# A hybrid decoder block on one core: the attention's value products in two halves of their PSUM bank, and a reordered head

## The chip, the core and the metric

The kernel runs on one core of a Trainium2 chip. A core has five engines that this text names: PE (TensorE, the matrix products; its weight loads, PEld, overlap them), DVE (VectorE), ACT (ScalarE), POOL (GpSimd) and SP, whose queue issues the transfers (DMAs). Matrix products are written to PSUM, a memory that this kernel uses in banks of 128 partitions x 512 fp32 values, and DVE and ACT read them there; the other tiles lie in SBUF. The metric is the device time in microseconds (us) of one execution, less is better.

## The reference

One layer on x of 1024 tokens x 1024 channels, in fp32. h = RMSNorm(x) is projected with one matrix `w_in` to some 13,900 columns, which feed three branches; each branch is projected back to 1024 channels, the three are weighted by sigmoid gates and summed, projected once more, added to x and normalised.

- Mamba-2 branch: a causal convolution over tokens of width 4 with SiLU gives x, B and C; step sizes dt = softplus(...); a scan in chunks of 128 tokens; a SiLU gate and an RMSNorm.
- Pooling branch: trailing means over 2, 4, 8, 16 tokens, a small linear map, a SiLU gate.
- Attention branch, 16 heads of 64, stick-breaking instead of a softmax:

```python
z = jnp.einsum('bhtd,bhsd->bhts', qb, kb) * scale
log_beta = log_sigmoid(z)
log_one_minus = where(causal, log_sigmoid(-z), 0.0)
later = lax.cumsum(log_one_minus, axis=3, reverse=True) - log_one_minus
att = where(causal, exp(log_beta + later), 0.0)
o = einsum('bhts,bhsd->bhtd', att, vb)      # then o * silu(gate)
```

## The kernel before, in words

Every fp32 product is made of parts: an operand is split into a high part (a rounding cast, ACT) and a low part (operand minus high, DVE), and the products high x high, high x low and low x high are summed in PSUM. The stages run one after the other: the head (convolution part, `conv_part`), attention (`attention_part`), the chunked scan, pooling, merge and output.

**The head.** `norm_in` normalises and transposes x to `hT` (eight tiles). `conv_gen(b)` projects one block of 256 columns to four PSUM tiles (two column tiles `ct` x two token halves), convolves each over tokens (ACT L684, three DVE instructions L689), and after the second half takes the SiLU: ACT sigmoid L692, then the product L693 on POOL, then a DMA. `zd_open` (L597, L598, DVE) splits the weights of the 32 step sizes; `dt_part` multiplies them with h and works out dt and its sums: in `conv_gen(1)` it is advanced twice (L621 to L638, then L642 to L651), and the rest, two transposes L656, a copy L658 and two DMAs, is run by `self.drain(dt)` right after. Afterwards `g_gen(1)` projects a gate block (ACT sigmoid L774, DVE product L775). From then on blocks are multiplied with seven products instead of eight (`seven_block`, L291), which needs sums of token halves: `seven_operands` (L230 to L249, DVE) makes them, and `t_split` splits each one (ACT copy L256, DVE subtraction L257). In the whole head the order on PE, DVE, POOL and ACT is that in which the program writes the instructions. The PSUM tiles of the projections rotate over two banks (`mm`) and three more (`mmx`); the first seven-product block begins in a bank that the third gate product L775 reads.

**Attention.** A unit is (pair of heads p, head hd, pair of query tiles ip), ip = 0 to 3, 64 units. For the two query tiles of a unit `stage_qk` makes the scores (L879 to L882), two sigmoids of them (ACT L883, L886), the running product over the keys from the end (DVE scan L888) and the weights (DVE L889); rows get longer with ip, up to 1024 keys. `stage_tr(u, jc)` transposes a 256 x 256 block of weights (L906) and splits it into the tile `attT` (ACT L908, DVE L909). `stage_av(u, jc)` multiplies it with v (L929), four products into 256 columns of the bank `av`: columns 0 to 255 for even ip, 256 to 511 for odd ip. After the last one of an odd ip the bank is emptied: ACT copies 64 of its partitions to `o` (L934), DVE adds the other 64 (L935), POOL multiplies with the gate `gt` (L936), a DMA stores it. The bank is then given to the next group (ip = 2 after 1, the next head's ip = 0 after 3).

The program writes PE's order out by hand: in unit m it places the scores of unit m + 1 at the first two steps, and after each step a share of projection work for later heads (`fill`), so that PE has work while ACT, DVE and POOL do theirs. A value step comes four transposes after its own (`late`). Per head there are ten of each; unit ip = 0 has two steps, then four, six and eight. The other engines' order in the attention is set by the scheduler of the framework, which also sets every wait between engines, from the tiles and the PSUM banks that instructions touch.

## Time and profile before

| what | value |
|---|---|
| median of 3 runs | 2102.17 us (2101.26 to 2102.92) |
| the profiled execution: time, span | 2102.4 us, 2100.6 us |
[...]
| PE busy | 2037.3 us, 97% |
| DVE, ACT, POOL busy | 1325.7, 947.4, 311.2 us |

The span is the time from the first to the last instruction. [...] Where a line of a profile names a releaser (`<-`), that instruction ended the wait. A merged line (`x3`) gives the start of the first and the time to the end of the last of so many instructions.

### The profile page before, as it was taken

The numbers are of one execution on the slowest core, as the hardware profiler recorded it, in microseconds if no ns is written. First come the engines' busy times: TensorE is split into PE (matmuls) and PEld (weight loads), VectorE is DVE, ScalarE is ACT, GpSimd is POOL, SyncE is SP. The second block draws the span as 40 slices with busy tenths as digits, with TensorE's granted clock in tenths as the row PEclk, the third lists the DMA queues.
The fourth block names the chain that finished last, engine by engine and source line by source line (L and its number), as shares of the span: only waits on it lengthen the run. The fifth ranks groups of instructions, "written<-read, shape, count | busy, mean of one in ns | idle before, by whom it ended". The sixth has DMA issues, their size and how long they took to land.

```text
span 2100.6 us, 29502 instructions
## 1 busy us (share of the span) xinstructions
PE 2037.3 (97%) x11312; PEld 1735.0 (83%) x11312; DVE 1325.7 (63%) x1821; ACT 947.4 (45%) x1921; POOL 311.2 (15%) x416
## 2 busy tenths in 40 slices
PE   8999999999999999999999899999999999999998
PEld 6878878788888788988887787777888888888898
DVE  6786888748667757665667736777747724425333
ACT  5343344335545545454545546666543413313131
POOL 3000000001111201010101124444200002221000
PEclk9999999999999899999999999999999999999999
DMA  5322233331121121211111165666563635433232
GB/s 197 103 86 100 91 110 113 134 114 49 46 66 39 48 66 56 60 57 58 53 59 53 61 185 190 208 198 195 164 211 128 215 99 171 143 128 110 81 131 81
DMA packets 116155, 233.99 MB, mean 111 GB/s; under 512 B 9776, under 2 KB 59696, under 8 KB 116016
## 3 DMA queue, kind: packets, MB, share of 16 engines
q1 hardware_dynamic: 116016, 232.12, 34.1%
q8 instruction: 89, 1.46, 0.3%
q14 instruction: 50, 0.41, 0.1%
HBM read 168.38 MB, written 63.70 MB: 110 GB/s over the span
## 4 chain that ended last, share of the span: by engine, by line
PE 78%; DVE 15%; ACT 3%; issue 3%; DMA 1%; DVEq 0%; POOL 0%; ACTq 0%; SPq 0%; POOLq 0%
PE mm L388 26%; PE mmx L388 14%; PE mm L397 12%; PE mmx L291 4%; DVE om L888 4%; PE mmx L397 4%; PE av L929 3%; DVE acc L350 3%; PE yd L1157 3%; PE tr L906 2%; PE mm L291 1%; DVE be L889 1%; PE yo L1160 1%; PE st L1163 1%; PE z L879 1%
## 5 line engine op out<-in xcount | busy, mean ns | idle before, releaser
L388 PE MATMUL mm<-hT,w 128*128 128x512 f32 x2232 | 590.2, 408 | 2.9 <-DVE hT L584 2.8
L388 PEld LDWEIGHTS mm<-hT,w 128*128 128x128 f32 x2232 | 409.7, 191 | 94.4 <-issue 15.1
L397 PE MATMUL mm<-w,hT 128*128 128x256 f32 x2112 | 291.2, 288 | 1.1 <-issue 1.1
L397 PEld LDWEIGHTS mm<-w,hT 128*128 128x128 f32 x2112 | 268.7, 193 | 1.8 <-issue 1.3
L388 PE MATMUL mmx<-x,w 128*128 128x512 f32 x1008 | 230.3, 389 | 0.0
L129 DVE TENSOR_TENSOR w<-raw,w 128x1024 fp32r<-128x1024 f32 x116 | 152.1, 1313 | 119.4 <-ACT w L128 119.1
L388 PEld LDWEIGHTS mmx<-x,w 128*128 128x128 f32 x1008 | 189.2, 188 | 39.3
L888 DVE TENSOR_TENSOR_SCAN om<-om,zero 128x128 f32<-128x128 f32 (+7 forms) x128 | 174.0, 1360 | 68.1 <-ACT om L883 67.2
L908 ACT CAST attT<-tr 128x512 fp32r<-128x512 f32 (+2 forms) x224 | 98.2, 438 | 159.9 <-PE tr L906 106.3
L909 DVE TENSOR_TENSOR attT<-tr,attT 128x512 fp32r<-128x512 f32 (+2 forms) x224 | 111.2, 497 | 91.2 <-ACT attT L908 90.0
L128 ACT CAST w<-raw 128x1024 fp32r<-128x1024 f32 x116 | 121.5, 1050 | 66.1 <-PE mmx L388 27.4
L883 ACT ACTIVATE om<-z 128x128 f32<-128x128 f32 (+2 forms) x192 | 92.5, 495 | 76.7 <-PE z L882 75.5
L388 PE MATMUL mm<-x,w 128*128 128x512 f32 x528 | 122.7, 389 | 0.0
L1286 ACT ACTIVATE gt<-gt 128x1024 f32<-128x1024 f32 x32 | 34.0, 1062 | 185.7 <-DMA gt<-d_gate 185.0
L388 PEld LDWEIGHTS mm<-x,w 128*128 128x128 f32 x528 | 99.1, 188 | 20.7
L388 PE MATMUL mmx<-hT,w 128*128 128x512 f32 x456 | 104.9, 390 | 0.0
L889 DVE TENSOR_TENSOR be<-be,om 128x128 f32<-128x128 f32 (+7 forms) x128 | 97.3, 760 | 11.9
L1134 POOL TENSOR_TENSOR E<-E,cbm 128x1024 f32<-128x1024 f32 x32 | 76.6, 2393 | 160.0 <-issue 104.8
L388 PEld LDWEIGHTS mmx<-hT,w 128*128 128x128 f32 x456 | 85.4, 188 | 17.6
L906 PE MATMUL tr<-cm,be 128*128 128x128 f32 x576 | 93.0, 280 | 0.5 <-DVE be L889 0.5
L886 ACT ACTIVATE be<-z 128x128 f32<-128x128 f32 (+2 forms) x192 | 92.5, 500 | 0.1
L870 POOL MEMSET om<- 128x1 f32 x128 | 12.6, 98 | 503.9 <-DVE be L889 405.1
(250 smaller groups left out, 3296.0 us busy)
## 6 DMA issues: line engine op xcount, KB each, us to landing
raw<-in_wblk SPq DMA_DIRECT2D x148, 512.0 KB, 4.1
E<-d_act SPq DMA_DIRECT2D x32, 512.0 KB, 4.8
gt<-d_gate SPq DMA_DIRECT2D x32, 512.0 KB, 3.9
d_gate<-mg SPq DMA_DIRECT2D x16, 512.0 KB, 4.0
xi<-d_x SPq DMA_DIRECT2D x32, 256.0 KB, 3.2
zs<-d_z SPq DMA_DIRECT2D x32, 256.0 KB, 2.7
d_ssm<-yt SPq DMA_DIRECT2D x32, 256.0 KB, 3.1
xraw<-d_ssm SPq DMA_DIRECT2D x16, 512.0 KB, 5.9
```

Of the source, the lines that this page charges most:

```text
L128: nc.scalar.copy(hi, raw)
L129: nc.vector.tensor_tensor(out=lo, in0=raw, in1=hi.bitcast(F32), op=ALU.subtract)
L291: T.matmul(ps, w[a](i, k), mov[b](j, k), start=first and n == 0, stop=n == 11, skip_group_check=not first)
L388: T.matmul(ps, w(a, k, ct * P, ct * P + P), mov(b, k, half * 512, half * 512 + 512), start=n == 0, stop=n == 23)
L397: T.matmul(ps, sta(a, k, tok * P, tok * P + P), w(b, k, 0, ncol), start=n == 0, stop=n == 23)
L883: A.activation(om[:, c0 : c0 + n], z[:, 0:n], AF.Sigmoid, scale=-0.125)
L886: A.activation(be[:, c0 : c0 + n], z[:, 0:n], AF.Sigmoid, scale=0.125)
L888: V.tensor_tensor_scan(out=rev, data0=rev, data1=self.zero.broadcast_to((P, L)), initial=1.0, op0=ALU.mult, op1=ALU.add)
L889: V.tensor_tensor(out=be[:, 0:L], in0=be[:, 0:L], in1=om[:, 1 : L + 1], op=ALU.mult)
L906: T.transpose(tr[:, c : c + P], b[:, (2 * jc + j) * P : (2 * jc + j + 1) * P], self.ident)
L908: A.copy(at[:, 0, sl], tr[:, sl])
L909: V.tensor_tensor(out=at[:, 1, sl], in0=tr[:, sl], in1=at[:, 0, sl].bitcast(F32), op=ALU.subtract)
```

## The change

- `t_split` only puts the low part's subtraction on a list; `t_flush` issues it, one or two instructions into the next token sum, at the first step of `conv_gen(1)`, or at step 50 of `g_gen(1)`.
- The SiLU product of `conv_gen` runs on DVE instead of POOL (four instructions).
- The last part of `dt_part` is run 15 products into `g_gen(1)` instead of ahead of it; the memory of `ws` is opened there.
- The bank `av` is one tile for the whole attention. Even ip write its first half and odd ip the second, and each half is emptied as soon as its own ip is complete (ACT copy and DVE addition of 256 columns, 64 times, instead of 512 columns, 32 times). `o` has two buffers and is taken at the first step of a group.
- A value step comes three transposes after its own instead of four, and `attT` has four buffers instead of five.

```diff
@@ -215,6 +215,7 @@
         self.tt = {i: pool.tile([P, 2, 4, 512], F32R, name=f"tt{i}") for i in (2, 3)}
         self.park = self.dram.tile([P, 4, 2, 512], F32, name="d_b12")
         self.t1, keep = {}, {}
+        self.t_late = []
         lo, hi = slice(0, 512), slice(512, 1024)
         f = lambda t, part, sl: t[:, part, sl].bitcast(F32)
 
@@ -229,6 +230,7 @@
             e = keep[k] = epool.tile([P, 512], F32, tag="te", name="te", bufs=2) if k < 2 else tmp("te")
             V.tensor_tensor(out=d, in0=f(a, 0, hi), in1=f(a, 0, lo), op=ALU.subtract)
             V.tensor_tensor(out=t1, in0=f(a, 1, hi), in1=f(a, 1, lo), op=ALU.subtract)
+            self.t_flush()
             V.tensor_tensor(out=t1, in0=t1, in1=d, op=ALU.add)
             V.tensor_tensor(out=e, in0=f(c, 0, hi), in1=t1, op=ALU.subtract)
             V.tensor_tensor(out=e, in0=e, in1=f(c, 1, hi), op=ALU.add)
@@ -238,6 +240,7 @@
             a, c = self.hT[k], self.hT[4 + k]
             d, e = tmp("td"), tmp("te")
             V.tensor_tensor(out=d, in0=f(c, 0, hi), in1=f(a, 0, hi), op=ALU.subtract)
+            self.t_flush()
             V.tensor_tensor(out=e, in0=f(c, 1, hi), in1=f(a, 1, hi), op=ALU.subtract)
             V.tensor_tensor(out=d, in0=d, in1=e, op=ALU.add)
             self.t_split(3, k, d)
@@ -246,6 +249,7 @@
             c = self.hT[4 + k]
             d, e = tmp("td"), keep.pop(k)
             V.tensor_tensor(out=d, in0=f(c, 0, lo), in1=e, op=ALU.subtract)
+            self.t_flush()
             V.tensor_tensor(out=d, in0=d, in1=f(c, 1, lo), op=ALU.add)
             self.t_split(4, k, d)
 
@@ -254,7 +258,11 @@
     def t_split(self, i, k, src):
         hi, lo = self.tt[i][:, 0, k], self.tt[i][:, 1, k]
         self.nc.scalar.copy(hi, src)
-        self.nc.vector.tensor_tensor(out=lo, in0=src, in1=hi.bitcast(F32), op=ALU.subtract)
+        self.t_late.append(lambda: self.nc.vector.tensor_tensor(out=lo, in0=src, in1=hi.bitcast(F32), op=ALU.subtract))
+
+    def t_flush(self):
+        while self.t_late:
+            self.t_late.pop(0)()
 
     def seven_first(self):
 
@@ -690,7 +698,7 @@
             if half == 1:
                 sg = pool.tile([P, S], F32, tag="csg", name="csg", bufs=2)
                 nc.scalar.activation(sg, acc[:, 0:S], AF.Sigmoid)
-                nc.gpsimd.tensor_tensor(out=sg, in0=sg, in1=acc[:, 0:S], op=ALU.mult)
+                nc.vector.tensor_tensor(out=sg, in0=sg, in1=acc[:, 0:S], op=ALU.mult)
                 dst = self.d_x[col // 4][:, col % 4] if col < 16 else self.d_bc[:, col - 16]
                 nc.sync.dma_start(out=dst, in_=sg)
             yield
@@ -730,18 +738,22 @@
                 if i in steps:
                     steps[i][0](steps[i][1])
             for i, _ in enumerate(self.conv_gen(1, pool)):
+                if i == 0:
+                    self.t_flush()
                 if i in (0, 2):
                     next(dt, None)
-            self.drain(dt)
-            dctx.close()
-            self.wspool = self.sb(ctx, "ws_sb", 2)
             self.wseven = {}
             steps = {4: (two, 2), 16: (one, 3), 32: (three, 3), 44: (two, 3)}
             prep = {}
             for i, _ in enumerate(self.g_gen(1)):
                 if i in steps:
                     steps[i][0](steps[i][1])
+                if i == 14:
+                    self.drain(dt)
+                    dctx.close()
+                    self.wspool = self.sb(ctx, "ws_sb", 2)
                 if i == 50:
+                    self.t_flush()
                     prep = self.seven_prep(BLK[SEVEN[0]])
                 if i > 50 and i % 8 == 0 and prep:
                     prep.pop(min(prep))()
@@ -850,7 +862,7 @@
             self.mmx = 0
             pz = self.ps(ctx, "a_z", 3)
             ptr = self.ps(ctx, "a_tr", 2)
-            pav = self.ps(ctx, "a_av", 1)
+            avs = self.ps(ctx, "a_av", 1).tile([P, 512], F32, name="av")
             qk, vv = {}, {}
             make = {"vz": lambda p: self.vz_gen(p, pool, vv), "qk": lambda p: self.qk_gen(p, pool, qk), "z": self.z_gen, "g": self.g_gen, "m": self.merge_gen}
             self.start_fill([(key, make[key[0]](key[1])) for key in [("vz", 0), ("qk", 0)] + sum(ATT_FILL, [])])
@@ -896,7 +908,7 @@
                 ip = u[2]
                 b0, b1 = state[u, 0], state[u, 1]
                 tr = ptr.tile([P, 512], F32, tag="tr", name="tr")
-                at = pool.tile([P, 2, 512], F32R, tag="attT", name="attT", bufs=5)
+                at = pool.tile([P, 2, 512], F32R, tag="attT", name="attT", bufs=4)
                 blocks = [(0, 0, b0), (0, 1, b1), (1, 0, b0), (1, 1, b1)]
                 if jc == ip:
                     blocks.pop(2)
@@ -917,24 +929,26 @@
                 rows = slice(64 * hd, 64 * hd + 64)
                 half = ip // 2
                 hs = slice(half * 512, half * 512 + 512)
-                if jc == 0 and ip % 2 == 0:
-                    gt = pool.tile([P, 512], F32, tag="gt", name="gt", bufs=1)
-                    nc.sync.dma_start(out=gt[rows], in_=self.d_g[rows, p, hs])
-                    av[0] = (pav.tile([P, 512], F32, tag="av", name="av"), gt)
-                ps, gt = av[0]
-                c = 256 * (ip % 2)
+                if jc == 0:
+                    if ip % 2 == 0:
+                        gt = pool.tile([P, 512], F32, tag="gt", name="gt", bufs=1)
+                        nc.sync.dma_start(out=gt[rows], in_=self.d_g[rows, p, hs])
+                        av[1] = (pool.tile([P, 512], F32, tag="o", name="o", bufs=2), gt)
+                ps = avs[:, 256 * (ip % 2) : 256 * (ip % 2) + 256]
+                o, gt = av[1]
                 n = 0
                 for j in range(2):
                     for part in range(2):
-                        T.matmul(ps[:, c : c + 256], v[:, 2 * jc + j], at[:, part, 256 * j : 256 * j + 256], start=jc == 0 and n == 0, stop=jc == ip and n == 3)
+                        T.matmul(ps, v[:, 2 * jc + j], at[:, part, 256 * j : 256 * j + 256], start=jc == 0 and n == 0, stop=jc == ip and n == 3)
                         n += 1
-                if jc == ip and ip % 2 == 1:
+                if jc == ip:
                     other = slice(64 - 64 * hd, 128 - 64 * hd)
-                    o = pool.tile([P, 512], F32, tag="o", name="o", bufs=1)
-                    A.copy(o[rows], ps[other])
-                    V.tensor_tensor(out=o[rows], in0=o[rows], in1=ps[rows], op=ALU.add)
-                    G.tensor_tensor(out=o[rows], in0=o[rows], in1=gt[rows], op=ALU.mult)
-                    nc.sync.dma_start(out=self.d_y["sb"][p // 4][rows, p % 4, hs], in_=o[rows])
+                    cs = slice(256 * (ip % 2), 256 * (ip % 2) + 256)
+                    A.copy(o[rows, cs], ps[other])
+                    V.tensor_tensor(out=o[rows, cs], in0=o[rows, cs], in1=ps[rows], op=ALU.add)
+                    if ip % 2 == 1:
+                        G.tensor_tensor(out=o[rows], in0=o[rows], in1=gt[rows], op=ALU.mult)
+                        nc.sync.dma_start(out=self.d_y["sb"][p // 4][rows, p % 4, hs], in_=o[rows])
 
             n = len(units)
             weight = [0.4 + 0.6 * (u[2] + 1) / 2.5 for u in units]
@@ -950,7 +964,7 @@
                 for jc in range(ip + 1):
                     subs.append((stage_tr, u, jc))
                     late.append((stage_av, u, jc))
-                    if len(late) > 4:
+                    if len(late) > 3:
                         subs.append(late.pop(0))
                 if m == n - 1:
                     subs += late
```

## Rows read from the trace of the kernel before

**Rows 1.** The page, part 1: busy time of each engine, share, instructions.

```profile
PE 2037.3 (97%) x11312; PEld 1735.0 (83%) x11312; DVE 1325.7 (63%) x1821; ACT 947.4 (45%) x1921; POOL 311.2 (15%) x416
```

**Rows 2.** Waits of PE, whole span: total us, times, longest us.

```profile
PE av L929 <- DVE o L935: 36.1, 16, 4.3
PE mm L291 <- DVE gsg L775: 2.9, 1, 2.9
...
PE mmx L656 <- DVE dt_all L643: 2.0, 1, 2.0
```

**Rows 3.** Timeline: start us, us, engine, line, operation [idle before <- releaser].

```profile
582.79 0.63 PE L929 MATMUL av<-attT,vb 128*128 128x256 f32 x4
...
584.42 2.29 DVE L888 TENSOR_TENSOR_SCAN om<-om,zero 128x1024 f32<-128x1024 f32 x1
...
584.64 0.58 ACT L934 COPY o<-av 64x512 f32<-64x512 f32 x1
...
586.84 1.23 DVE L889 TENSOR_TENSOR be<-be,om 128x1024 f32<-128x1024 f32 x1
588.09 0.69 DVE L935 TENSOR_TENSOR o<-o,av 64x512 f32<-64x512 f32 x1
...
588.84 0.74 PE L929 MATMUL av<-attT,va 128*128 128x256 f32 x4 [1.88 <-DVE o L935]
```

**Rows 4.** Waits of all engines in the attention, 480 to 1240 us.

```profile
ACT attT L908 <- DVE attT L909: 51.3, 50, 2.9
...
ACT vb L792 <- DVE va L791: 24.8, 21, 3.6
```

**Rows 5.** Groups by line and form, attention: count | busy us, mean ns | idle before.

```profile
L909 DVE TENSOR_TENSOR attT<-tr,attT 128x256 fp32r<-128x256 f32 x63 | 26.4, 420 | 45.9 <-ACT attT L908 45.8
...
L883 ACT ACTIVATE om<-z 128x256 f32<-128x256 f32 x46 | 17.8, 386 | 25.4 <-PE z L882 25.1
```

**Rows 6.** Windows: busy us (instructions) of PE, PEld, DVE, ACT, POOL; clock; DMA; GB/s.

```profile
480.00:1240.00 760.00, 722.53 (x4687) 642.31 (x4686) 504.85 (x695) 391.62 (x868) 104.73 (x244) 0.97 0.20 58
...
590.00:600.00 10.00, 10.00 (x74) 9.91 (x73) 3.64 (x10) 3.41 (x11) 0.63 (x3) 0.83 0.20 54
```

**Rows 7.** Timeline of the head, 114 to 177 us.

```profile
114.76 2.60 DVE L129 TENSOR_TENSOR w<-raw,w 128x1024 fp32r<-128x1024 f32 x1 [3.35 <-ACT w L128]
...
122.22 2.32 DVE L689 SCALAR_TENSOR_TENSOR cacc<-mm,cols,cacc 128x510 f32<-128x510 f32 x3 [0.24 <-ACT cacc L684]
...
125.93 1.06 ACT L692 ACTIVATE csg<-cacc 128x1024 f32<-128x1024 f32 x1
...
127.07 2.40 POOL L693 TENSOR_TENSOR csg<-csg,cacc 128x1024 f32<-128x1024 f32 x1 [10.81 <-ACT csg L692]
127.54 2.48 DVE L257 TENSOR_TENSOR tt<-td,tt 128x512 fp32r<-128x512 f32 x1 [0.74 <-ACT tt L256]
...
134.08 0.69 DVE L257 TENSOR_TENSOR tt<-te,tt 128x512 fp32r<-128x512 f32 x1 [0.69 <-ACT tt L256]
...
145.17 4.74 PE L291 MATMUL mm<-hT,w 128*128 128x512 f32 x12 [2.90 <-DVE gsg L775]
...
149.74 2.97 PE L291 MATMUL mm<-tt,w 128*128 128x512 f32 x12
...
176.24 1.23 DVE L335 TENSOR_TENSOR cx<-cx,acc 128x1024 f32<-128x1024 f32 x1 [0.61 <-ACT cx L353]
```

**Rows 8.** Timeline of the head, around the first step-size product.

```profile
45.66 0.28 DVE L597 CAST zd<-wdt_raw 128x256 fp32r<-128x256 f32 x1
...
45.98 0.43 DVE L598 TENSOR_TENSOR zd<-wdt_raw,zd 128x256 fp32r<-128x256 f32 x1
47.11 1.06 ACT L692 ACTIVATE csg<-cacc 128x1024 f32<-128x1024 f32 x1
...
47.85 3.35 PE L397 MATMUL mmx<-zd,hT 128*128 128x288 f32 x24
```

**Rows 9.** Timeline of a head in which DVE took the addition first.

```profile
1206.98 0.65 DVE L935 TENSOR_TENSOR o<-o,av 64x512 f32<-64x512 f32 x1
```

## What was predicted

> **What bounds the kernel now.** I read the busy times first: PE works 2037.3 of 2100.6 us [rows 1], so only its 63 us of idle time, and the time it runs at the lower clock, are to be had. Then PE's waits over the whole span, because they say who makes it idle. One wait is 36.1 us in 16 times: the value products (L929) wait for the DVE addition that empties their PSUM bank (L935). The other two that the change touches lie in the head: 2.0 us for the copy L643 ahead of the transposes L656, and 2.9 us for a gate product (L775) ahead of the first seven-product block [rows 2]. Third, the timeline around one of the 16 waits, to see what makes the emptying late.
>
> There the last value products of a group end at 582.79 + 0.63 = 583.42, right after the score products of the longest unit (ip = 3). ACT copies at 584.64. DVE, however, holds the scan (584.42, 2.29 us) and its multiplication (586.84, 1.23 us) of that same long unit, and takes the addition only at 588.09. PE starts again at 588.84 after 1.88 us idle [rows 3]. So the price is DVE's queue, not the addition itself. Placing all 32 releases in the timeline: 15 of the 16 waits (34.8 us together, 1.7 to 4.3 us each) are this very place, once per head, in the unit ip = 2, where PE asks for the bank 3.5 us after the last product and gets it 5.3 us after. The sixteenth (1.3 us) is the release between ip = 1 and ip = 2.
>
> **The change part by part. The bank in two halves.** Written out, the order is: with the lag of three, unit ip = 2 now runs score products, transposes, score products, value products of ip = 0, transposes, value products of ip = 1. So the place behind the long scans falls to the step from ip = 0 to ip = 1, that is from half A to half B. The release from ip = 3 to the next ip = 0 moves one unit earlier, ahead of the long scans, where PE leaves at least 4 us between the two and DVE is free after about 2; it costs nothing. The other two releases (ip = 1 to 2, ip = 2 to 3) leave 2.0 us and more in all heads but the last three, against an emptying of under 2 us: nothing either.
>
> Everything now hangs on whether a product into half B must wait for the emptying of half A. No row of before shows PE beside a reader of the same bank. The nearest rows show two readers: ACT's copy L792 reads other columns of the bank and writes another tile than DVE's L791, shares no element with it, and yet waits 24.8 us for it in 21 times; L908 waits 51.3 us for L909 of other columns [rows 4]. The program orders accesses by bank, not by column. I take it that it does so for PE too; then the wait is not removed, it is handed to the other half.
>
> [...]
>
> The cost under that reading: the addition shrinks from 0.69 us to about 0.42 (the same engine's 256-column form) [rows 5], so each of 15 waits loses 0.26 us: -3.9. The 1.3 us wait goes: -1.3. Head 0 had no release at this place and gets one: +1.8 (between 0 and 2.9, the range of the others but the two longest). Idle time: -3.4. The 32 more copies and additions, at most 386 and 420 ns each [rows 5], lie on ACT and DVE beside PE's filling work; nothing, and they would cost only in the last three heads, where the fill runs out.
>
> The clock: the granted clock is 1.00 in most ten-microsecond rows of the attention and 0.97 over its 760 us, a loss of 20.5 us by the finer rows; all of it lies next to these waits. The wait of 1.88 us is followed by a row at 0.83, which is 1.7 us of work lost [rows 6]; others of nearly that length by none. Of the waits up to 1.8 us, 1 in 4 was followed by a fall, of those of 1.9 to 2.0 us 4 in 6, of the longer ones all. Nine waits move from the second group and the top of the first into 1.4 to 1.8 us: some three falls fewer, -5, and +1 for head 0's: -4 (between +2 and -12). Sum of the attention: -7.4.
>
> The shorter lag: an `attT` tile is read three steps after its transposes instead of four, still over 9 us, against 5 us in the slowest of its splits; nothing. The second `o` buffer lets ACT write while the last one is on its way out; ACT was not waiting for that. The gate load `gt` on SP waits for POOL's product of the last group, which is now done a unit earlier; nothing or a gain for SP.
>
> **The SiLU products of the token convolution, POOL to DVE.** Four instructions. On DVE one costs 1.23 us (L335, same shape); POOL took 2.40 [rows 7]. The point is what is queued behind it on DVE, since all engines here keep program order. In the first block it stands in front of L597 and L598, which split the step-size weights. Now L598 starts at 45.98 and PE takes these weights at 47.85 without a wait [rows 8]. After, DVE must first wait for the sigmoid, which ends at 47.11 + 1.06 = 48.17, then 1.23 + 0.28 + 0.43 us follow: L598 ends at 50.1 and PE idles from 48.0: **+2.1 us**, a new wait (1.5 to 2.5, by how much of the three overlaps).
>
> **The head from there to the first seven-product block.** The transposes L656, their copy and their two DMAs on SP move 15 products, some 3.5 us, into the next gate block, past the copy L643 that they waited 2.0 us for: that wait goes, and the DMAs are read only in the scan stage. But PE then arrives at the seven-product block at 145.17 - 2.90 - 2.0 = 140.3, and still needs the bank that the third L775 frees at 145.1 [rows 7]. I followed DVE's queue to that L775 in the new order:
> - a subtraction moved into the step-size chain: +0.2;
> - the first product fits a pause in which DVE waited for ACT: +0.3;
> - POOL no longer slows two splits, which took 2.60 and 2.48 us while it ran its product, against 1.23 and 0.69 [rows 7]: -1.4 and -1.8;
> - the second product has to wait for the sigmoid, which ends at 126.99, 2.4 us after its input (L689, 122.22 + 2.32) [rows 7], while the token sums that used to fill that time stand behind it: 2.4 + 1.2 less overlaps, +3.4;
> - the deferred subtraction saves DVE's 0.7 us wait for ACT's copy [rows 7] twice, -1.4, and loses half a microsecond twice, where a gate product follows at once and waits for the same ACT, +1.0.
>
> Together the third L775 comes 0.3 us later (-1 to +2.8, if POOL's hold is not given back) in a frame that is itself 2.1 us late. So the waits of 2.0 and 2.9 us become one of 5.2: **+2.4 us** for the head. The clock: after the 2.9 us wait twelve products took 4.74 us and the next twelve 2.97 [rows 7]; a wait of 5.2 will cost as much or double, and the one at 48 may cost a fall too: +1.6 (0 to 3.4). Sum of the head: +4.0.
>
> **The sum.** -7.4 + 4.0 = -3.4. The profiled execution took 2102.4 us (span 2100.6), 0.2 above the median of the runs; 2102.4 - 3.4 = 2099.0, and I give that.
>
> **The rivals.**
> *DVE's order turns.* DVE is ordered by the scheduler in the attention, not by hand. In three of the 15 heads it set the addition ahead of the scan's multiplication (1206.98) [rows 9]. There ACT's copy ended 2.1 us or more before the scan did, in the twelve others 1.2 to 1.8 us. The narrower copy gains 0.2 us (0.58 to 0.386) [rows 3, 5]: typically 1.7, nearest to the twelve, so I leave the order. If it turns, 12 waits lose up to 1.23 us more (-15), head 0's too (-1), and some eight falls of the clock (-9): 2074.
>
> *The halves are independent after all.* If the order went by columns, half A would have three value steps to be emptied: 36.1 us and the 20.5 us of clock go, the head's 4.0 stay: 2050. Against it: [rows 4].
>
> *The head wins over the attention.* One mechanism: the product on DVE waits for ACT's sigmoid and holds up what is queued behind. Its price is 2.1 us at 48, up to 2.8 at the seven-product block, and a clock fall at each, 3.4: 8.3. If the attention keeps all its falls of the clock and gets one for head 0, it gives only 3.4 - 1: +6, 2108. It decides from an attention gain under 4 us.
>
> **How the numbers follow.** Forecast, the wait stays behind the scans: 0.56 (own range 2091 to 2106). DVE's order turns: 0.23. Head wins: 0.14. Independent halves: 0.07. The range leaves out the last, the lowest quarter of the second and the edges: 2072 to 2109. A measurement of this kernel tells some 0.2% (4.2 us) from no change. Faster: 0.07 + 0.23 + 0.22 of the forecast's own = 0.52; within: 0.30; slower: 0.14 + 0.04 = 0.18.
>
> **What would show it.** Right: value products still wait for the addition, some 16 times, 30 to 34 us in all, at the second value step of the unit ip = 2; a new PE wait of 2 us for L598's split near 48; no wait ahead of L656; one of about 5 us ahead of the first seven-product block. Wrong: no PE wait on the addition (independent halves), waits of 0.4 us with the addition ahead of the multiplication (order turned), or no wait near 48.

## The result, and the profile after

The kernel after takes **2077.34 us** (median of 4 runs, 2075.85 to 2078.43) against 2102.28 us for the kernel before on the same chip: a ratio of 0.9881, interval 0.9864 to 0.9898. Its profiled execution has a span of 2074.7 us, 25.9 less than before, at a granted clock (the share of PE's full speed, as the profile gives it) of 0.991 over the span against 0.987. The forecast was 2099.0; 2077 lies near the lower end of its range and 3 us from the rival "DVE's order turns", 2074. Of all executions behind the times below one stands apart: one of the 11 of the SiLU products alone took 3385.6 us at a granted clock of 0.58 and is left out of its ratio. In the kernel after the value products are L942, ACT's copy L947, the addition L948, the scan L900, its multiplication L901, the gate product L787, the seven products L299, the two splits of the step-size weights L605 and L606, and the step-size product L405.

The waits of PE over the whole span (total us, times, longest us), which answer [rows 2]:

```profile
PE av L942 <- DVE o L948: 18.3, 14, 3.0
PE mm L299 <- DVE gsg L787: 5.3, 1, 5.3
...
PE mmx L405 <- DVE zd L605: 1.7, 1, 1.7
```

The wait on the addition is halved, neither kept at 30 to 34 us nor gone. The two other lines are the head's, and as forecast: one wait of 5.3 us ahead of the seven-product block where there had been 2.0 and 2.9, and a new one for the step-size weights.

The timeline of the head that [rows 3] shows (start us, us, engine, line, operation, idle time before and its releaser), the same place after the change:

```profile
585.08 0.63 PE L942 MATMUL av<-attT,va 128*128 128x256 f32 x4
585.85 1.08 DVE L901 TENSOR_TENSOR be<-be,om 128x896 f32<-128x896 f32 x1
586.85 2.28 DVE L900 TENSOR_TENSOR_SCAN om<-om,zero 128x1024 f32<-128x1024 f32 x1
586.93 0.37 ACT L947 COPY o<-av 64x256 f32<-64x256 f32 x1
...
589.05 0.39 DVE L948 TENSOR_TENSOR o<-o,av 64x256 f32<-64x256 f32 x1
589.36 1.21 DVE L901 TENSOR_TENSOR be<-be,om 128x1024 f32<-128x1024 f32 x1
...
589.49 0.74 PE L942 MATMUL av<-attT,va 128*128 128x256 f32 x4 [0.24 <-DVE o L948]
```

Two things are to be read here. The products that wait at 589.49 write half B, and they are released by the addition that empties half A: the halves are not independent. And DVE takes the addition straight after the scan, ahead of the multiplication that stood in front of it before. I followed the release in all 16 heads: every head has it at this step, ip = 0 to ip = 1, and every head has this order. Thirteen of the 14 waits, 17.8 of the 18.3 us, lie there; the other, 0.5 us, is a release from ip = 1 to ip = 2. Ten heads wait 0.7 us or less; the six others wait 1.6 to 3.0 us, since there the long scan starts 1.9 us or more after the products' end (1.14 us in the head shown).

The stretch of the attention and the head, from the windows (busy us and instructions of PE, PEld, DVE, ACT, POOL; clock; DMA share; GB/s). After:

```profile
480.00:1240.00 760.00, 738.53 (x4842) 655.50 (x4840) 526.61 (x750) 418.82 (x955) 107.09 (x251) 0.99 0.22 67
...
590.00:600.00 10.00, 10.00 (x88) 9.91 (x87) 6.37 (x16) 4.24 (x13) 1.73 (x4) 1.00 0.19 54
...
0.00:480.00 480.00, 462.79 (x2202) 380.63 (x2202) 348.90 (x488) 192.11 (x288) 22.25 (x50) 0.98 0.34 116
```

Before, the head:

```profile
0.00:480.00 480.00, 463.67 (x2215) 380.74 (x2216) 350.65 (x486) 192.62 (x293) 32.11 (x56) 0.99 0.33 116
```

PE's idle time is the window less its busy time; what the clock costs is the sum of (1 - granted clock) over the ten-microsecond rows of the stretch.

| us | before | after | difference |
|---|---|---|---|
| idle, 480 to 1240 | 37.5 | 21.5 | -16.0 |
| clock, 480 to 1240 | 20.5 | 6.8 | -13.7 |
| idle, 0 to 480 | 16.3 | 17.2 | +0.9 |
| clock, 0 to 480 | 5.1 | 8.5 | +3.4 |

Together -25.4, against 25.9 us of span. The ten microseconds behind the wait, at 0.83 before [rows 6], are at 1.00 now; in the attention 4 such rows are below 1.00 after, 15 before. Of the +3.4 of the clock ahead of 480 us, half lies between 10 and 30 us, before the change does anything; the other half is the fall behind the seven-product block (140 to 160 us: 1.7 before, 3.4 after).

The head around the two new waits, from the timeline after, beside [rows 8] and [rows 7]:

```profile
47.12 1.06 ACT L700 ACTIVATE csg<-cacc 128x1024 f32<-128x1024 f32 x1
...
48.21 1.22 DVE L701 TENSOR_TENSOR csg<-csg,cacc 128x1024 f32<-128x1024 f32 x1 [2.46 <-ACT csg L700]
49.35 0.28 DVE L605 CAST zd<-wdt_raw 128x256 fp32r<-128x256 f32 x1
...
49.69 0.40 PE L405 MATMUL mmx<-zd,hT 128*128 128x288 f32 x1 [1.68 <-DVE zd L605]
50.24 1.03 PE L405 MATMUL mmx<-zd,hT 128*128 128x288 f32 x6 [0.15 <-DVE zd L606]
...
146.92 0.68 DVE L787 TENSOR_TENSOR gsg<-gsg,mm 128x512 f32<-128x512 f32 x1
...
147.66 4.73 PE L299 MATMUL mm<-hT,w 128*128 128x512 f32 x12 [5.26 <-DVE gsg L787]
```

The sigmoid, the product, the two splits and PE stand in one chain, as worked out. The gate product that frees the bank ends at 147.60; the forecast had it 2.4 us behind 145.1, at 147.5.

### The profile page after: what moved, and what is told of

It is laid out like the page before. It is cut to its first block, busy times and chain, and to the rows that moved or that the text cites. A ratio compares the mean times of both kernels' runs of the same rounds, so it can differ in the third digit from the quotient of the medians.

```text
span 2074.7 us, 29592 instructions
## 1 busy us (share of the span) xinstructions
PE 2026.5 (98%) x11312; PEld 1726.4 (83%) x11312; DVE 1333.1 (64%) x1857; ACT 952.4 (46%) x1953; POOL 292.5 (14%) x412
## 4 chain that ended last, share of the span: by engine, by line
PE 78%; DVE 15%; ACT 4%; issue 3%; DMA 1%; DVEq 0%; POOL 0%; ACTq 0%; SPq 0%; POOLq 0%
PE mm L396 27%; PE mmx L396 14%; PE mm L405 12%; PE mmx L299 4%; DVE om L900 4%; PE mmx L405 4%; PE av L942 3%; DVE acc L358 3%; PE yd L1171 3%; PE tr L918 2%; PE mm L299 1%; PE yo L1174 1%; PE st L1177 1%; DVE be L901 1%; PE z L891 1%
## 5 line engine op out<-in xcount | busy, mean ns | idle before, releaser
L396 PE MATMUL mm<-hT,w 128*128 128x512 f32 x2232 | 584.3, 405 | 1.9 <-DVE hT L592 1.8
L405 PE MATMUL mm<-w,hT 128*128 128x256 f32 x2112 | 287.9, 286 | 2.0 <-issue 1.1
L405 PEld LDWEIGHTS mm<-w,hT 128*128 128x128 f32 x2112 | 265.1, 191 | 3.4 <-ACT qb L835 1.6
L900 DVE TENSOR_TENSOR_SCAN om<-om,zero 128x128 f32<-128x128 f32 (+7 forms) x128 | 175.5, 1372 | 61.8 <-ACT om L895 60.9
L901 DVE TENSOR_TENSOR be<-be,om 128x128 f32<-128x128 f32 (+7 forms) x128 | 98.1, 767 | 10.5
L1309 POOL TENSOR_TENSOR acc<-acc,gt 128x512 f32<-128x512 f32 x32 | 45.6, 1426 | 247.0 <-DVE gt L1308 125.9
```

The source lines that it names most:

```text
L396: T.matmul(ps, w(a, k, ct * P, ct * P + P), mov(b, k, half * 512, half * 512 + 512), start=n == 0, stop=n == 23)
L405: T.matmul(ps, sta(a, k, tok * P, tok * P + P), w(b, k, 0, ncol), start=n == 0, stop=n == 23)
L900: V.tensor_tensor_scan(out=rev, data0=rev, data1=self.zero.broadcast_to((P, L)), initial=1.0, op0=ALU.mult, op1=ALU.add)
L901: V.tensor_tensor(out=be[:, 0:L], in0=be[:, 0:L], in1=om[:, 1 : L + 1], op=ALU.mult)
```

## The experiments

All ratios are against the kernel before, run on the same chip in turn with the kernel; its median was 2100.6 us beside the head alone, the attention alone, the old order and the lag of three; 2101.55 beside the order alone, the narrow copy, the lag of four and the early split; and 2101.86 beside the SiLU products and the last two. My theory after the result was: what pays is DVE's order, addition ahead of multiplication, and it turned because ACT's copy became shorter; the halves by themselves free nothing, and the head costs what was forecast.

### The head alone

The kernel before with all of the diff outside the attention: the late subtractions (`t_late`, `t_flush`), the SiLU products on DVE, the move of the step-size chain's rest.

```
-        self.nc.vector.tensor_tensor(out=lo, in0=src, in1=hi.bitcast(F32), op=ALU.subtract)
+        self.t_late.append(lambda: self.nc.vector.tensor_tensor(out=lo, in0=src, in1=hi.bitcast(F32), op=ALU.subtract))
...
-                nc.gpsimd.tensor_tensor(out=sg, in0=sg, in1=acc[:, 0:S], op=ALU.mult)
+                nc.vector.tensor_tensor(out=sg, in0=sg, in1=acc[:, 0:S], op=ALU.mult)
```

> The head's part of the change alone, attention as before. Theory (the gain is all in the attention, the head costs): the attention keeps its waits of some 36 us and its clock loss of some 20 us; the head shows the new wait of 1.9 us near 49, no wait ahead of the transposes of the step sizes and one of 5.3 us ahead of the first seven-product block, with one more fall of the clock: 2102 + 4 = 2106 (2104 to 2108). Rival (the reordered head gives time): 2100 or less.

Measured: 2103.97 us (10 runs), ratio 1.0015 (1.0005 to 1.0024): +3.4 us between the medians. The profile has the waits of 5.3 and 1.7 us, and its attention still waits 36.0 us in 16 times. The forecast for the head, +4.0, holds in the sum.

### The attention alone

The rest of the diff: halves, two `o` buffers, four `attT` buffers, lag of three.

```
-            pav = self.ps(ctx, "a_av", 1)
+            avs = self.ps(ctx, "a_av", 1).tile([P, 512], F32, name="av")
...
-                    if len(late) > 4:
+                    if len(late) > 3:
```

> The attention's part of the change alone, head as before. Theory: waits of the value products for the addition 18 us in all as in the changed kernel, addition ahead of the long multiplication in all heads: 2077 - 4 = 2073. Rival (the head has a share in the gain): 2078 or more.

Measured: 2074.67 us, ratio 0.9878 (0.9862 to 0.9893): -25.9 us, with the same 18.3 us in 14 times. The gain is all in the attention.

### The halves with DVE's old order

```
-                V.tensor_tensor(out=be[:, 0:L], in0=be[:, 0:L], in1=om[:, 1 : L + 1], op=ALU.mult)
+                mul[0] = V.tensor_tensor(out=be[:, 0:L], in0=be[:, 0:L], in1=om[:, 1 : L + 1], op=ALU.mult)
...
-                    V.tensor_tensor(out=o[rows, cs], in0=o[rows, cs], in1=ps[rows], op=ALU.add)
+                    with tc.issue_after(mul[0].ins):
+                        V.tensor_tensor(out=o[rows, cs], in0=o[rows, cs], in1=ps[rows], op=ALU.add)
```

The kernel after, with each addition queued behind the last multiplication.

> The changed kernel with each addition of a half kept behind the last multiplication of the weights that was written before it, on DVE; nothing else. Theory (the prediction's miss is DVE's order alone): waits of 30 to 34 us at the step from ip = 0 to ip = 1, most of the clock loss back: 2095 to 2101. Rival (the halves or the lag give the time, whatever DVE's order): 2075 to 2080.

Measured: 2109.34 us, ratio 1.0044 (1.0029 to 1.0058). The waits of PE and the place in the timeline:

```profile
PE av L943 <- DVE o L950: 40.7, 17, 4.8
```

```profile
592.00 2.28 DVE L901 TENSOR_TENSOR_SCAN om<-om,zero 128x1024 f32<-128x1024 f32 x1
592.09 0.37 ACT L948 COPY o<-av 64x256 f32<-64x256 f32 x1
...
594.42 1.22 DVE L902 TENSOR_TENSOR be<-be,om 128x1024 f32<-128x1024 f32 x1
595.57 0.41 DVE L950 TENSOR_TENSOR o<-o,av 64x256 f32<-64x256 f32 x1
...
596.03 0.74 PE L943 MATMUL av<-attT,va 128*128 128x256 f32 x4 [1.62 <-DVE o L950]
```

With this order nothing of the gain is left, so the order carries it. The head shown waits 1.62 us where the forecast had 1.88 less 0.26. But the kernel is slower than the 2095 to 2101 us that I had expected: in the six heads with the late scan the waits are 3.0 to 4.8 us. The edit also forces the three heads that had the addition first of themselves in the kernel before, which adds 4.3 us of waits there. So this is not quite my likeliest case. Forced in every head the attention costs about 5.3 us (2109.34 less the head's 3.4, against 2100.6); less those 4.3 us, which is an estimate, it is near the time of before and not at -7.4.

### The order alone, without halves

```
-                V.tensor_tensor(out=be[:, 0:L], in0=be[:, 0:L], in1=om[:, 1 : L + 1], op=ALU.mult)
                 state[u, ii] = be
+                return lambda: V.tensor_tensor(out=be[:, 0:L], in0=be[:, 0:L], in1=om[:, 1 : L + 1], op=ALU.mult)
...
+                    if mult and add:
+                        with tc.issue_after(add.ins):
+                            mult()
```

The kernel before; where a scan's multiplication and an addition are issued together, the multiplication is queued behind the addition. In every unit it is also written one call later, behind the transposes or value products of its step. Bank and lag stay: whole bank, lag of four.

> The kernel before, with DVE's order turned and nothing else: the long multiplication of the weights is queued behind the addition that empties the bank, in every head; bank, lag and head are as before. Theory (DVE's order is what gave the time): the 12 waits of 1.7 to 2 us shrink by the multiplication's 1.23 us, 36 us of waits become some 21, the clock loss falls from 20 us to under 10: 25 us faster than before on the same chip (20 to 30). Rival (the halves or the shorter lag give the time): within 5 us of before.

Measured: 2075.14 us, ratio 0.9875 (0.986 to 0.989). The waits and the timeline:

```profile
PE av L929 <- DVE o L935: 20.1, 16, 2.9
```

```profile
580.69 2.28 DVE L888 TENSOR_TENSOR_SCAN om<-om,zero 128x1024 f32<-128x1024 f32 x1
580.91 0.58 ACT L934 COPY o<-av 64x512 f32<-64x512 f32 x1
583.00 0.69 DVE L935 TENSOR_TENSOR o<-o,av 64x512 f32<-64x512 f32 x1
583.75 0.74 PE L929 MATMUL av<-attT,va 128*128 128x256 f32 x4 [0.52 <-DVE o L935]
```

The place of one instruction in DVE's queue gives as much as the whole attention part of the change (0.9878). The wait of 1.88 us is 0.52: the multiplication's 1.23 us and a little more.

### Why the order turned: the copy's width

```
-                    A.copy(o[rows], ps[other])
-                    V.tensor_tensor(out=o[rows], in0=o[rows], in1=ps[rows], op=ALU.add)
+                    A.copy(o[rows, 0:256], ps[other, 0:256])
+                    h2 = lambda t: t.rearrange("p (a b) -> p a b", a=2)
+                    V.tensor_tensor(out=h2(o[rows])[:, ::-1], in0=o[rows, 0:256].unsqueeze(1).broadcast_to((64, 2, 256)), in1=h2(ps[rows])[:, ::-1], op=ALU.add)
```

The kernel before with ACT's copy alone narrowed to 256 columns; the addition stays 512 wide and takes the copied columns twice. The kernel leaves out the other half of the copy.

> The kernel before, with ACT's copy out of the bank at 256 columns instead of 512; the addition stays at 512 and takes the copied columns twice, so the other half of the copy is left out. Theory (the narrower copy is what turns the scheduler's order of addition and multiplication): the addition stands ahead of the long multiplication in the heads, and the time is that of the run with the turned order, within 4 us. Rival (the copy's width only saves its own 0.2 us): within 4 us of before.

Measured: 2077.13 us, ratio 0.9884 (0.9869 to 0.9898), 20.5 us of waits in 17 times. The timeline:

```profile
579.27 2.29 DVE L888 TENSOR_TENSOR_SCAN om<-om,zero 128x1024 f32<-128x1024 f32 x1
579.49 0.36 ACT L934 COPY o<-av 64x256 f32<-64x256 f32 x1
...
581.59 0.69 DVE L936 TENSOR_TENSOR o<-o,av 64x512 f32<-64x512 f32 x1
582.31 1.23 DVE L889 TENSOR_TENSOR be<-be,om 128x1024 f32<-128x1024 f32 x1
```

ACT's copy takes 0.36 us in place of 0.58 (0.37 in the kernel after), and DVE's order turns, with the whole bank and a lag of four. So the copy's length decides which of the two the scheduler sets first, unless the addition's other operands do, which had to change with it (its time, 0.69 us, did not); on the chip the copy had ended 1.5 us before the scan in the kernel before too [rows 3].

### The halves with the lag of four

The attention part of the diff without its last hunk (`len(late) > 4` kept), and with five `attT` buffers and one `o` buffer as before. The lines below are the edit against the kernel after.

```
-                        av[1] = (pool.tile([P, 512], F32, tag="o", name="o", bufs=2), gt)
+                        av[1] = (pool.tile([P, 512], F32, tag="o", name="o", bufs=1), gt)
...
-                    if len(late) > 3:
+                    if len(late) > 4:
```

> The two halves, emptied for each pair of query tiles, with the lag of four and one buffer for the output rows as before; head as before. Theory (the shorter lag does nothing in the change, as it only brings another step to the place behind the scans): waits of 17 to 20 us, now at the step from ip = 3 to ip = 0, and 2072 to 2077 as with the whole attention part. Rival (the shorter lag gives the time in the change): 2095 or more.

Measured: 2104.79 us (10 runs), ratio 1.0018 (1.0009 to 1.0027). The forecast of 2072 to 2077 fell, but the run does not settle why, since it holds back two things, the lag and the second `o` buffer.

```profile
PE av L930 <- DVE o L936: 39.1, 27, 2.9
```

```profile
587.41 2.29 DVE L888 TENSOR_TENSOR_SCAN om<-om,zero 128x1024 f32<-128x1024 f32 x1
587.63 0.36 ACT L935 COPY o<-av 64x256 f32<-64x256 f32 x1
589.73 0.42 DVE L936 TENSOR_TENSOR o<-o,av 64x256 f32<-64x256 f32 x1
590.18 1.23 DVE L889 TENSOR_TENSOR be<-be,om 128x1024 f32<-128x1024 f32 x1
590.20 0.74 PE L930 MATMUL av<-attT,va 128*128 128x256 f32 x4 [0.25 <-DVE o L936]
...
594.91 0.37 ACT L935 COPY o<-av 64x256 f32<-64x256 f32 x1 [1.97 <-DMA d_sb<-o]
595.32 0.41 DVE L936 TENSOR_TENSOR o<-o,av 64x256 f32<-64x256 f32 x1 [1.92 <-ACT o L935]
...
595.78 0.74 PE L930 MATMUL av<-attT,va 128*128 128x256 f32 x4 [1.30 <-DVE o L936]
```

The addition comes first here too, and the wait at the release from ip = 3 is the same 0.25 us. But PE waits at the next release as well, from ip = 0 to ip = 1: summed over the heads 14.0 us at the first and 23.9 at the second. The second wait is not DVE's queue behind the scan. The rows show what it is: ACT's copy into `o` waits for the DMA that still stores the last group out of the one `o` buffer. In 13 heads, with 17.9 of the 23.9 us, the copy starts within 0.1 us of that store's landing. In the kernel after, with two buffers and the emptying of ip = 3 one unit earlier, the store has landed before the copy in 14 of 15 heads. Which of the two changes takes this wait away, and so what the lag of three is worth to the halves, no run here shows.

### The lag of three alone

```
-                    if len(late) > 4:
+                    if len(late) > 3:
```

> The kernel before with the shorter lag alone (a value step three transposes after its own); the bank stays whole and is emptied 32 times. Theory: no release falls behind the long scans any more, since the one from ip = 3 to the next ip = 0 moves ahead of them; the 36 us of waits nearly all go (under 4 us left) and with them most of the 20 us of clock loss: 2048 (2045 to 2058). Rival (the gain needs the two halves): 2098 to 2104, with waits of some 30 us.

Measured: 2059.67 us, ratio 0.9804 (0.9789 to 0.9818), faster than both kernels. The waits, the window and the longest wait left:

```profile
PE av L929 <- DVE o L935: 8.0, 5, 2.8
```

```profile
480.00:1240.00 760.00, 748.26 (x4921) 665.42 (x4920) 536.84 (x730) 421.02 (x946) 112.10 (x251) 1.00 0.24 71
```

```profile
720.82 1.22 DVE L129 TENSOR_TENSOR w<-raw,w 128x1024 fp32r<-128x1024 f32 x1
722.07 0.69 DVE L829 TENSOR_TENSOR kb<-mm,kb 64x512 fp32r<-64x512 f32 x1
722.79 0.69 DVE L935 TENSOR_TENSOR o<-o,av 64x512 f32<-64x512 f32 x1
...
723.63 0.70 PE L929 MATMUL av<-attT,vb 128*128 128x256 f32 x4 [2.82 <-DVE o L935]
```

With the whole bank there are only two releases in a head, and a lag of three sets neither of them behind the long scans. The release from ip = 3 waits nowhere, and the one from ip = 1 to 2 in five heads; in the longest, shown here, splits of weights and keys stand ahead of the addition. That is 8.0 us where I had expected under 4, and the time is 12 us above the 2048 I gave: the direction was right, the size was not. The halves thus cost a part of what the lag alone brings: the attention part of the change, which has the same lag and the halves, took 2074.67 us on the same chip, 15 us more.

### The two parts of the head

The split of the step-size weights one step earlier, in the kernel after:

```
             for i, _ in enumerate(self.conv_gen(0, pool, norm)):
-                if i == 2:
+                if i == 1:
                     self.zd_open(dpool)
```

> The changed kernel, with the split of the step-size weights one PSUM tile earlier, ahead of the first SiLU product in DVE's queue. Theory: the 1.9 us wait near 49 goes, all else in the head comes as much earlier, the 5.3 us wait at the first seven-product block stays: 2 us faster than the changed kernel, 4 with a fall of the clock. Rival (the wait is given back at the seven-product block): same time, that wait 7 us.

Measured: 2075.18 us, ratio 0.9876 (0.986 to 0.9893). The wait of 1.7 us is gone, the one of 5.3 us stays. The intervals of this kernel and of after overlap, so that the 2 us can't be told from nothing.

The SiLU products alone, in the kernel before:

```
-                nc.gpsimd.tensor_tensor(out=sg, in0=sg, in1=acc[:, 0:S], op=ALU.mult)
+                nc.vector.tensor_tensor(out=sg, in0=sg, in1=acc[:, 0:S], op=ALU.mult)
```

> The kernel before with only the four SiLU products of the token convolution moved from POOL to DVE. Theory (DVE keeps the order of its program, and what stands behind the product waits for ACT's sigmoid): a new PE wait of about 1.9 us near 49 for the second split of the step-size weights, the wait ahead of the step-size transposes about 1.1 us instead of 2.0, the wait ahead of the first seven-product block about 4.5 us instead of 2.9; together some 2.6 us slower than before, ratio about 1.0012. Rival (the products on POOL held DVE's splits up, so that taking them off POOL pays for the rest): no slower than before, with the wait ahead of the seven-product block not longer than 2.9 us.

Measured: 2104.73 us (11 runs), ratio 1.0016 (1.0006 to 1.0025): +2.9 us where 2.6 was worked out. The waits of PE:

```profile
PE mm L291 <- DVE gsg L775: 4.8, 1, 4.8
...
PE mmx L397 <- DVE zd L597: 1.7, 1, 1.7
...
PE mmx L656 <- DVE dt_all L643: 0.9, 1, 0.9
```

So the move of the product to DVE is nearly all of the head's price. What the reordering of the token sums and the moved step-size chain add to it can't be told from nothing: the ratios are 1.0016 here and 1.0015 for the whole head, and the two waits sum to 5.7 us here and 5.3 after.

### The shorter lag, with the head's wait taken off DVE

The lag of three once more, to stand beside it on one chip:

> The kernel before with the shorter lag of the value products alone (three steps instead of four), once more, to stand beside the next kernel on the same chip: 2058 to 2061 us, 8 us of PE waits for the addition.

Measured: 2058.99 us, ratio 0.9796 (0.9782 to 0.9809).

```
-            steps = {8: (three, 0), 24: (three, 1), 48: (one, 2), 72: (three, 2)}
+            steps = {8: (three, 0), 24: (three, 1), 48: (one, 2), 72: (three, 2), 84: (two, 2)}
...
-            self.drain(dt)
-            dctx.close()
-            self.wspool = self.sb(ctx, "ws_sb", 2)
...
-            steps = {4: (two, 2), 16: (one, 3), 32: (three, 3), 44: (two, 3)}
+            steps = {16: (one, 3), 32: (three, 3), 44: (two, 3)}
...
+                if i == 14:
+                    self.drain(dt)
+                    dctx.close()
+                    self.wspool = self.sb(ctx, "ws_sb", 2)
```

> The shorter lag alone, and in the head of before two moves: the rest of the step-size chain runs 15 products into the second gate block (past the copy that PE waited 2.0 us for), and the token sum that stood at step 4 of that block goes to step 84 of the first one, where DVE idled for some 3 us. The SiLU products stay on POOL. Theory (the wait ahead of the first seven-product block is DVE's backlog, and the sum moved into an idle stretch takes 1.2 us or more off it): the wait of 2.0 us goes, the one ahead of the block, otherwise 4.9, stays under 3; 2 to 5 us faster than the shorter lag alone, 2055 to 2058. Rival (the backlog only moves): the wait of 2.0 us goes and the one ahead of the block grows by as much; the same time as the shorter lag alone within 1 us.

Measured: **2055.58 us**, ratio 0.9781 (0.9767 to 0.9794), the fastest of all; its runs (2055.18 to 2057.02) lie below all of the lag alone (2057.52 to 2060.49). The waits of PE in the head:

```profile
PE mm L291 <- DVE gsg L776: 2.0, 1, 2.0
```

The wait of 2.0 us ahead of the step-size transposes is gone, and the one ahead of the block is 2.0 where the lag alone has 2.9. With one token sum moved into a stretch where DVE idled, the third gate product starts at 141.27, against 144.00 and 144.31 in the two runs of the lag alone, so that the backlog was made shorter and not only moved.

## Why the prediction missed by 22 us

**What bounds the kernel.** Right: the wait on the addition is DVE's queue and not the addition. The two experiments on the order show it from both sides, 0.9875 with the order turned in the kernel before and 1.0044 with the old order forced on the kernel after.

**Do the halves free each other?** Right: no. The release of half B's products by half A's addition stands in the timeline after. In the kernel after PE waited 17.8 us for the emptying of other columns of the same bank. What the products would do without that wait, no run here shows.

**Where the wait falls.** Right: the step from ip = 0 to ip = 1 in the unit ip = 2, head 0 included (1.6 us for 1.8). The releases that I set at nothing cost 0.5 us in one head. But I read the halves with the lag as one edit, and they pull against each other: the lag without halves gives -2.0%, both -1.2%. The prediction never worked out the lag by itself (its paragraph "The shorter lag" looks at the buffers alone): it is worth 41 us without the halves, since it moves a release away from the long scans. What it is worth with them stays open, since the run with the lag of four had one `o` buffer as well. That buffer I set at nothing ("ACT was not waiting for that"); with halves and the lag of four ACT does wait for it, for 1.1 to 2.3 us in the ten heads where the trace names the store.

**DVE's order.** This is the step that failed: "typically 1.7, nearest to the twelve, so I leave the order". The mechanism was written down as a rival, with the right cause (the narrower copy) and nearly the right time, at 0.23. The choice went wrong by the measure I took: I sorted heads by when ACT's copy ended before the scan in the executed trace, and put 1.7 us between 1.2 to 1.8 and 2.1. But the order is made by the scheduler when the program is built, and the trace shows only its outcome. The kernel after shows how little that measure says: the copy ends 1.4 to 2.8 us before the scan, and the addition comes first at 1.4 as at 2.8. A margin of 0.4 us between heads of either order was no ground for leaving the twelve others at better than two to one. The rival's sum came out: the twelve waits fell by 18.1 us together (its 15, and 3.1 for the narrower addition), the three that had the order before by 0.3, and head 0 has a new wait of 1.6. The measured time lies in the range because the range took this rival in; the forecast itself had the other order.

**The size of the likeliest case.** Also too hopeful, as far as the forced order can tell. It leaves 40.7 us of waits, or 36.4 (an estimate) without the 4.3 that it adds in three heads, where 30 to 34 were forecast. The ten waits of 1.7 to 2.0 us shrank by 0.15 us on average instead of 0.26, the two longest by 0.15 us or less, and head 0 got 3.0 us instead of 1.8.

**The clock.** It followed the waits: 13.7 us less in the attention. The rival had -9 on top of the -4 of the forecast, together 13. The loss does not go by the sum of the waits alone: the halves with the lag of four have 39.1 us of them, more than before, but none above 2.9 us, and lose 12.0 us to the clock in the attention, against 20.5 before.

**The head.** Right in each wait (1.7 and 0.15 for 2.1; none ahead of the transposes; 5.3 for 5.2) and in the sum, +3.4 measured alone for +4.0 (its interval reaches from 1 to 5 us). The clock's 1.6 is less sure. Behind the seven-product block the clock took 1.7 us more after than before, but no more than before in the profile of the head alone (1.7 in both), and the new wait at 49 us was followed by no fall. The price of 2.9 us in the old head is not firm either: in three runs with that head the clock fell at 120 us already, and the wait was 1.3 us.

## What to carry to other kernels

Where a scheduler orders an engine's queue, a shorter or longer instruction next to a tight place can turn that order, and the turn can be worth more than the edit (here 0.22 us off a copy turned it, and the kernel with that copy alone was 24.4 us faster); look at the order of the queue before asking what an edit costs, and write the order down by hand if it pays. Count the releases of a buffer and look at what each stands behind: a buffer split in two that is still guarded as one doubles the releases and frees nothing, as the 17.8 us of waits after show. Leave one thing at a time out of a change: with two left out, the lag and a buffer, a run could not say which of them mattered. Try the parts of a change one by one, the smallest first: here the last line of the diff, alone, gave more than all of it.

## What the runs showed of the hardware

In the head of the kernel before three DVE instructions began while POOL ran a SiLU product and took both operands from SBUF, and all three took longer than elsewhere: a split of a token sum 2.48 us against 0.69, a split of weights 2.60 against 1.23 [rows 7], and another of weights, at 53.34 us, 2.61. With the lag of three and the moved token sum it is another instruction, L234, 2.77 us where it took 0.69 in the lag of three alone:

```profile
126.74 0.69 DVE L233 TENSOR_TENSOR te<-hT,t 128x512 f32<-128x512 f32 x1
126.98 2.71 POOL L693 TENSOR_TENSOR csg<-csg,cacc 128x1024 f32<-128x1024 f32 x1 [10.81 <-ACT csg L692]
127.47 2.77 DVE L234 TENSOR_TENSOR te<-te,hT 128x512 f32<-128x512 f32 x1
```

With the products on DVE the split of weights that took 2.60 us [rows 7] takes 1.22. The subtraction L909, which has one operand in PSUM, shows no such difference: in the kernel before 23 of the 128x512 ones began while POOL multiplied `o`, and took 0.69 us on average, as the 73 others did. And it was not always DVE's instruction that took longer: at 538.72 and 727.86 us of the kernel before a split of weights beside POOL's product of `o` took its usual 1.21 us, and the product 2.79 us instead of 1.29; at 504.76 us the split took 1.52 us and the product 1.42. Giving back 1.4 and 1.8 us in this way still did not pay for a product that waits for ACT with all of DVE's queue behind it: with the SiLU products alone moved the kernel was 2.9 us slower.

What stays open: why six heads start the long scan later than the others, what the halves give with two `o` buffers and the lag of four, and whether an order of DVE's queue written out by hand on top of the shorter lag would take away the 8.0 us that are left.
